# Experts taken in an order that the chip sorts by their tokens, four of them in blocks of 64 tokens

## The chip, the core and the metric

The kernel runs on one core of a Trainium2 chip. The metric is device time in microseconds (us) for one execution, taken as the median over runs.

## What is computed

A float32 network of two blocks over 256 tokens of width 1024. The first block has two layers of a token mixer and a feed-forward part; the feed-forward part of the second layer is a mixture of eight experts, of which each token takes two. All that the change touches lies there:

```python
def _moe(h, w_router, w_gate, w_up, w_down):          # h: 256 tokens x 1024
    logits = (h @ w_router).astype(jnp.float32)
    top_val, top_idx = lax.top_k(logits, TOP_K)        # TOP_K = 2 of N_EXPERTS = 8
    ...
    for e in range(N_EXPERTS):                         # w_gate[e], w_up[e]: 1024 x 2816
        out = out + gates[..., e:e + 1] * _swiglu(h, w_gate[e], w_up[e], w_down[e])
```

`_swiglu` is `(silu(h @ w_gate) * (h @ w_up)) @ w_down`. All weights lie in HBM in float32: 3 x 1024 x 2816 x 4 bytes, 34.6 MB, for each expert.

## The kernel before

**Split operands.** Every float32 operand of a large product is split into a rounded part (`hi`, the type float32r) and the rest (`lo`). A product is then three matmuls into one PSUM bank (`mm3`, L383 to L386): hi by hi, hi by lo, lo by hi. The weights are split when they arrive: ScalarE casts `whi` from the raw tile (L368), VectorE subtracts and writes `wlo` (L370). There are four buffers of each, and one holds two pieces of 128x512 elements; a piece is 256 KB in HBM, and an expert has 132 of them.

**Loads.** SP issues all weight loads on one queue, one behind the other: `fetch` (L290, tiles of 1 MB, `raw`) and `rows_of` (L303, four single pieces of 256 KB, `rawrow`, in buffers that other stages leave free). A load waits until VectorE has split what its buffer held before. Nine loads are asked for before the router runs.

**The experts.** `moe` runs the router, then `prepare(e)` and the expert's products for e = 0 to 7, in that order, for every expert with room for 128 tokens. `route` builds a one-hot matrix `oh` from each token's place in its expert (`R`) and gathers the tokens by matmul (`pgat`, L1279); `prepare` splits them (`xehl`, `xehi`, `xelo`). `hidden` takes the 2816 columns in six groups (five of 512, one of 256): eight steps of 128 rows by three matmuls for gate and again for up (`pgu`), silu, product (`eh`), four transposes (`phT`) and a split (`ehh`, `ehl`). The tokens' split parts are what the array holds and the weights stream through it, so a matmul's length doesn't depend on how many of the 128 tokens are used. `combine` multiplies by the down weights, 2 halves of 22 steps by three matmuls (`pe`), and puts the result back by the transposed one-hot matrix (`psc`). The next expert is prepared in the midst of `hidden` (`then`). The scheduler of the framework places the instructions on each engine.

**More than 128 tokens.** If an expert has more than 128 tokens (`cint`, read by all engines, L1385), a loop over all eight experts (L1387) computes what is left over.

Of the kernel before, what the change touches and what calls it, by code (L numbers as in the profile page):

```python
# [9 lines left out]
F32 = mybir.dt.float32  # L10
F32R = mybir.dt.float32r
# [8 lines left out]
FF = 2816  # L20
# [12 lines left out]
SPREAD = "rcrmrcrmr"  # L33

# [28 lines left out]
def tile_hybrid_stack(ctx: ExitStack, tc: tile.TileContext, a, out, stages=STAGES):  # L63
# [34 lines left out]
    def small(shape, dt=F32, name="s", tag=None):  # L98
        n = 1
        for v in shape[1:]:  # L100
            n *= v
        tag = tag or ("s8" if n <= 8 else "s64" if n <= 64 else "s256")
        bufs = {"s8": 24, "s64": 8, "s256": 3, "kpe": 2, "adac": 10, "adaA": 3, "moe": 2, "moeb": 1, "dtv": 4, "pick": 3,
                "cint": 1}[tag]
        return sm.tile(shape, dt, tag=tag, bufs=bufs, name=nm(name))
# [124 lines left out]
    gp.memset(nones, -1.0)  # L230
    anti = cmat("anti", 1.0, 0.0, [[1, 128]], ALU.is_equal, -127, 1)
# [51 lines left out]
    lent = [False]  # L283

    def fetch(src, r0, nk, c0, n, tag=None):
        if tag is None:
            turn[0] += 1
            tag = "rawb" if turn[0] % 5 in (1, 3) and isinstance(src.offset, int) and not lent[0] else "rawa"
# [19 lines left out]
    def raw_tile(src, r0, nk, c0, n):  # L308
        if isinstance(src.offset, int):
# [30 lines left out]
    def wkey(src, r0, nk, c0, n):  # L340
        return src.tensor.name, src.offset, r0, nk, c0, n
# [846 lines left out]
    def moe(A, B, grow, before_branch):  # L1188
        wg, wu, wd = a["moe_w_gate"][0], a["moe_w_up"][0], a["moe_w_down"][0]
        for e in range(NE):  # L1190
            for c0 in range(0, FF, 512):
                for src in (wg, wu):
                    n = min(512, FF - c0)
                    reqs(src[e], 8, c0, n, STEP[n])
            for hf in range(2):
                reqs(wd[e], FF // P, hf * 512, 512, 4)
# [51 lines left out]
        cint = small([128, 1], I32, name="cint", tag="cint")  # L1248

        def gates():  # L1250
# [11 lines left out]
            cmax = small([128, 1], name="cmax")  # L1262
            vec.tensor_reduce(cmax, pr[:, 2, :], axis=AX.X, op=ALU.max)
            vec.tensor_copy(cint, cmax)

        def route(rcol, gcol, base, more=None):

            oh = pt([128, 2, 128], name="oh")
            for t in range(2):
                vec.tensor_scalar(oh[:, t, :], iota, float(base), rcol(t), op0=ALU.add, op1=ALU.is_equal)  # L1270
# [3 lines left out]
            for b in range(2):  # L1274
                ps = bank((128, 4, 128), "pgat", "o")
# [5 lines left out]
                f = pt([128, 4, 128], name="xe")  # L1281
# [20 lines left out]
        def prepare(e):  # L1302
            oht, gs, fulls = route(lambda t: R[:, t, e:e + 1], lambda t: G[:, t, e:e + 1], 0,
                                  None if e else gates)
            if e % 2:
                return oht, gs, [split(f, [128, 4, 128], "xe") for f in fulls]
# [7 lines left out]
            return oht, gs, xe  # L1314

# [30 lines left out]
        def combine(src, hs, oht, gs):  # L1346
# [23 lines left out]
        for e in range(NE):  # L1370
# [7 lines left out]
            hs = hidden((wg[e], wu[e]), cur[2], then)  # L1378
            combine(wd[e], hs, cur[0], cur[1])
# [5 lines left out]
        most = nc.values_load(cint[0:1, 0:1], min_val=0, max_val=256)  # L1385
        with tc.If(most > 128):
            with tc.For_i(0, NE, 1) as e:  # L1387
                oht, gs, fulls = route(lambda t: R[:, t, 0:1], lambda t: G[:, t, 0:1], 128)
# [4 lines left out]
                for c in (R, G):  # L1393
# [3 lines left out]
                    vec.tensor_copy(c, nx)  # L1397

# [595 lines left out]
```

## Time and profile before

| | |
|---|---|
| median of 3 runs | 2044.44 us (2044.15 to 2050.39) |
| the profiled execution | 2050.83 us, its span 2049.1 us |
| busy in the span: TensorE, VectorE, ScalarE | 1975.2, 1634.5, 1272.8 us |
| moved by DMA | 496.33 MB, mean 242 GB/s |

The span runs from the first to the last instruction. In the profile PE is TensorE's matmuls, DVE VectorE, ACT ScalarE, POOL GpSimd, SPq the queue of SyncE; L368 is a line of the kernel. A busy share over the span is a mean over stages with different limits, so the stage of the experts is looked at by itself.

### The profile page before, as it was taken

The numbers are of one execution on the slowest core, as the hardware profiler recorded it, in microseconds if no ns is written. First come the engines' busy times: TensorE is split into PE (matmuls) and PEld (weight loads), VectorE is DVE, ScalarE is ACT, GpSimd is POOL, SyncE is SP. The second block draws the span as 40 slices with busy tenths as digits, with TensorE's granted clock in tenths as the row PEclk, the third lists the DMA queues.
The fourth block names the chain that finished last, engine by engine and source line by source line (L and its number), as shares of the span: only waits on it lengthen the run. The fifth ranks groups of instructions, "written<-read, shape, count | busy, mean of one in ns | idle before, by whom it ended". The sixth has DMA issues, their size and how long they took to land. (4 is left out here: it accounts for less than half of the span.)

```text
span 2049.1 us, 32577 instructions
## 1 busy us (share of the span) xinstructions
PE 1975.2 (96%) x12095; PEld 1733.4 (85%) x12095; DVE 1634.5 (80%) x2629; ACT 1272.8 (62%) x1962; POOL 131.5 (6%) x207
## 2 busy tenths in 40 slices
PE   6989999998999999999999999989999889999999
PEld 6868998785788888888888888879998779999997
DVE  7888888775699999999999999877668567556783
ACT  2564444456488888788888888755555556545662
POOL 2310000022000000000000000012012000000000
PEclk9998999999899999999999999999999989999999
DMA  9726989662399999999999989845534324554552
GB/s 319 246 92 237 316 306 337 210 196 82 128 327 365 336 371 331 363 329 372 324 379 325 381 313 383 315 126 172 160 124 146 102 74 133 171 183 161 186 167 101
DMA packets 281353, 496.33 MB, mean 242 GB/s; under 512 B 16394, under 2 KB 64852, under 8 KB 281188
## 3 DMA queue, kind: packets, MB, share of 16 engines
q1 hardware_dynamic: 276900, 491.79, 69.1%
q10 hardware_dynamic: 3648, 2.14, 0.4%
q8 instruction: 97, 1.59, 0.3%
q0 software_dynamic: 640, 0.26, 0.1%
q14 instruction: 68, 0.56, 0.1%
HBM read 493.06 MB, written 1.06 MB: 241 GB/s over the span
## 5 line engine op out<-in xcount | busy, mean ns | idle before, releaser
L370 DVE TENSOR_TENSOR wlo<-raw,whi 128x1024 fp32r<-128x1024 f32 (+1 forms) x621 | 749.4, 1219 | 210.0 <-ACT whi L368 202.8
L368 ACT CAST whi<-raw 128x1024 fp32r<-128x1024 f32 (+1 forms) x621 | 647.6, 1048 | 382.8 <-PE pf L480 151.3
L478 PE MATMUL pf<-hhi,whi 128*128 128x256 f32 x1248 | 358.0, 287 | 0.5 <-ACT bc L1646 0.5
L481 PE MATMUL pf<-hhi,wlo 128*128 128x256 f32 x1248 | 357.0, 287 | 0.8 <-DVE wlo L370 0.7
L480 PE MATMUL pf<-hlo,whi 128*128 128x256 f32 x1248 | 356.2, 286 | 0.0
L368 ACT CAST whi<-rawrow 128x512 fp32r<-128x512 f32 x428 | 244.0, 620 | 51.6 <-PE pgu L386 25.6
L370 DVE TENSOR_TENSOR wlo<-rawrow,whi 128x512 fp32r<-128x512 f32 x428 | 270.5, 686 | 0.1
L478 PEld LDWEIGHTS pf<-hhi,whi 128*128 128x128 f32 x1248 | 240.5, 193 | 6.9 <-issue 4.8
L481 PEld LDWEIGHTS pf<-hhi,wlo 128*128 128x128 f32 x1248 | 239.7, 193 | 5.6 <-issue 3.7
L480 PEld LDWEIGHTS pf<-hlo,whi 128*128 128x128 f32 x1248 | 240.6, 193 | 1.8 <-issue 1.5
L385 PE MATMUL pgu<-wlo,xehi 128*128 128x512 f32 (+1 forms) x384 | 144.1, 376 | 0.9 <-DVE wlo L370 0.9
L385 PE MATMUL pgu<-wlo,xehl 128*128 128x512 f32 (+1 forms) x384 | 144.6, 376 | 0.0
L386 PE MATMUL pgu<-whi,xehl 128*128 128x512 f32 (+1 forms) x384 | 142.9, 373 | 0.0
L386 PE MATMUL pgu<-whi,xelo 128*128 128x512 f32 (+1 forms) x384 | 142.7, 372 | 0.0
L384 PE MATMUL pgu<-whi,xehi 128*128 128x512 f32 (+1 forms) x384 | 139.0, 374 | 1.4 <-ACT whi L368 1.4
L384 PE MATMUL pgu<-whi,xehl 128*128 128x512 f32 (+1 forms) x384 | 139.6, 374 | 0.0
L385 PE MATMUL pe<-wlo,ehh 128*128 128x512 f32 x352 | 138.0, 392 | 0.1
L386 PE MATMUL pe<-whi,ehl 128*128 128x512 f32 x352 | 137.1, 389 | 0.0
L384 PE MATMUL pe<-whi,ehh 128*128 128x512 f32 x352 | 136.5, 392 | 0.0
L532 DVE SCALAR_TENSOR_TENSOR acc<-raw,ccol,acc 128x512 f32<-128x512 f32 x164 | 121.9, 749 | 6.7 <-DMA raw<-in_ada_w_dram 4.8
L384 PE MATMUL pt<-whi,hhi 128*128 128x256 f32 (+2 forms) x384 | 115.3, 302 | 0.0
L386 PE MATMUL pt<-whi,hlo 128*128 128x256 f32 (+2 forms) x384 | 114.8, 299 | 0.0
(512 smaller groups left out, 3709.8 us busy)
## 6 DMA issues: line engine op xcount, KB each, us to landing
raw<-in_w_in_dram SPq DMA_DIRECT2D x62, 1024.0 KB
raw<-in_moe_w_up_dram SPq DMA_DIRECT2D x53, 1024.0 KB
raw<-in_moe_w_gate_dram SPq DMA_DIRECT2D x51, 1024.0 KB
raw<-in_moe_w_down_dram SPq DMA_DIRECT2D x45, 1024.0 KB
raw<-in_ada_w_dram SPq DMA_DIRECT2D x44, 1024.0 KB
rawrow<-in_moe_w_gate_dram SPq DMA_DIRECT2D x148, 256.0 KB
rawrow<-in_moe_w_up_dram SPq DMA_DIRECT2D x140, 256.0 KB
rawrow<-in_moe_w_down_dram SPq DMA_DIRECT2D x140, 256.0 KB
```

What stands on the lines that cost most here:

```text
L368: behind("hi", nc.scalar.copy(hi[:, i, :], r), 2)
L370: behind("lo", vec.tensor_sub(lo[:, i, :], r, hi.bitcast(F32)[:, i, :]), 2)
L384: mm(ps, lh, wh, start=first, stop=False, skip_group_check=True)
L385: mm(ps, lh, wl, start=False, stop=False, skip_group_check=True)
L386: mm(ps, ll, wh, start=False, stop=last, skip_group_check=True)
L478: mm(o, wh[j][:, s], X.h(kc), start=(kc == 0 and ch % 2 == 0), stop=False, skip_group_check=True)
L480: mm(o, wh[j][:, s], X.l(kc), start=False, stop=False, skip_group_check=True)
L481: mm(o, wl[j][:, s], X.h(kc), start=False, stop=(kc == KC - 1), skip_group_check=True)
L532: behind("ada", vec.scalar_tensor_tensor(acc, raws[k], ccol[:, k:k + 1], acc, op0=ALU.mult, op1=ALU.add))
```

## The change

Expert 0 is computed first, as before. Its routing gives the number of tokens of each expert, and some 30 small VectorE operations rank experts 1 to 7 by it (`turns_of_experts`). They are then computed in the order of ranks 3, 0, 4, 1, 5, 2, 6 (`TURNS`; rank 0 has the most tokens), so that an expert of the four with the fewest tokens and one of the three with the most take turns. SP reads the seven numbers into registers, and each load of these experts takes its address from such a register.

The four experts of rank 3 to 6 ("light") have room for 64 tokens. The rounded part and the rest of their tokens lie side by side in one operand of 128 columns, so that two matmuls (by `whi` and by `wlo`, `doubled`) stand for three, and rows 0 to 63 and 64 to 127 of the result are two halves that have yet to be added. ScalarE copies each gate and up bank out of PSUM (`eg`), and TensorE adds the halves and transposes in one matmul by a matrix `fold` (128x64, two unit matrices on top of each other). For the down product the same two matmuls are used, and the one-hot matrix, which holds each token twice, adds the halves when it puts tokens back. The loop for what is left over now runs if a heavy expert has more than 128 tokens or a light one more than 64.

```diff
+TURNS = (3, 0, 4, 1, 5, 2, 6)
+HEAVY = 3
...
+    fold = const.tile([128, 64], F32, name="fold")
+    gp.tensor_add(fold, ident[:, 0:64], ident[:, 64:128])
...
-        for e in range(NE):
+        def announce(g, u, d):
...
+        mine = [(wg[0], wu[0], wd[0])]
+        announce(*mine[0])
...
+        def turns_of_experts():
+
+            N = NE - 1
+            cnt = small([128, 8], name="cnt", tag="order")
+            vec.tensor_copy(cnt, pr[:, 2, :])
+            key = small([128, N], name="key", tag="order")
+            vec.scalar_tensor_tensor(key, cnt[:, 1:8], 8.0, iota[:, 1:8], op0=ALU.mult, op1=ALU.subtract)
...
+            vec.tensor_reduce(rank, cube, axis=AX.X, op=ALU.add)
+
+            for i, k in enumerate(TURNS):
+                vec.tensor_scalar(cube[:, i, :], rank, float(k), None, op0=ALU.is_equal)
...
+            vec.tensor_copy(cint[:, 1:8], who)
...
+            vec.tensor_sub(over[:, 1:8], cnt[:, 1:8], rank)
...
+            for t in range(2):
+                vec.tensor_scalar(Rx[:, t, 0:1], R[:, t, 0:1], -128.0, None, op0=ALU.add)
+                vec.tensor_sub(Rx[:, t, 1:8], R[:, t, 1:8], rank)
+                for o, v in ((Rt, R), (Gt, G)):
+                    vec.tensor_tensor(prod, cube, v[:, t, None, 1:8].to_broadcast([128, N, N]), op=ALU.mult)
+                    vec.tensor_reduce(o[:, t, 1:8], prod, axis=AX.X, op=ALU.add)
+            for i in range(N):
+                e = nc.values_load(cint[0:1, i + 1:i + 2], engines=[mybir.EngineType.SP], min_val=0, max_val=NE - 1)
+                mine.append([w[bass.ds(e, 1)].rearrange("o k n -> (o k) n") for w in (wg, wu, wd)])
+                announce(*mine[-1])
...
-        def route(rcol, gcol, base, more=None):
+        def route(rcol, gcol, more=None, n=128):
...
-                        mm(ps[:, i, :], xn[t][:, kc * P:(kc + 1) * P], oh[:, t, :], start=(t == 0),
+                        mm(ps[:, i, :], xn[t][:, kc * P:(kc + 1) * P], oh[:, t, 0:n], start=(t == 0),
...
+            if light(k):
+                oht, gs, fulls = route(lambda t: Rt[:, t, k:k + 1], lambda t: Gt[:, t, k:k + 1], None, 64)
+                xe = []
+                for f in fulls:
+                    hl = pt([128, 4, 128], F32R, "xel")
+                    nc.scalar.copy(hl[:, :, 0:64], f)
+                    vec.tensor_sub(hl[:, :, 64:128], f, hl.bitcast(F32)[:, :, 0:64])
+                    xe.append(hl)
+                return oht, gs, xe
...
+        def light(k):
+            return k and TURNS[k - 1] >= HEAVY
+
+        def doubled(ps, n, hl, wh, wl, j, kc, KC):
+
+            o = hl[kc // 4][:, kc % 4, :]
+            mm(ps[:, :n], o, wh[j], start=(kc == 0), stop=False, skip_group_check=True)
+            mm(ps[:, :n], o, wl[j], start=False, stop=(kc == KC - 1), skip_group_check=True)
+
+        def hidden_light(srcs, xe, then):
...
+                            doubled(ps, n, xe, wh, wl, j, k0 + j, 8)
+                    o = pt([128, 512], name="eg")
+                    nc.scalar.copy(o[:, :n], ps[:, :n])
+                    both.append(o)
+
+                pT = bank((128, 2, 4, 64), "phT", "t")
+                for k in range(2):
+                    for i in range(m):
+                        mm(pT[:, k, i, :], both[k][:, i * P:(i + 1) * P], fold, start=True, stop=True)
+                s = pt([128, 4, 64], name="eh")
+                act(s[:, :m, :], pT[:, 0, :m, :], AF.Silu)
+                vec.tensor_mul(s[:, :m, :], s[:, :m, :], pT[:, 1, :m, :])
+                hl = pt([128, 4, 128], F32R, "ehhl")
+                nc.scalar.copy(hl[:, :m, 0:64], s[:, :m, :])
+                vec.tensor_sub(hl[:, :m, 64:128], s[:, :m, :], hl.bitcast(F32)[:, :m, 0:64])
...
+                        if few:
+                            doubled(ps, 512, hs, wh, wl, j, kc, FF // P)
+                            continue
...
-            hs = hidden((wg[e], wu[e]), cur[2], then)
-            combine(wd[e], hs, cur[0], cur[1])
+            g_, u_, d_ = mine[e]
+            hs = (hidden_light if light(e) else hidden)((g_, u_), cur[2], then)
+            combine(d_, hs, cur[0], cur[1], light(e))
...
-        most = nc.values_load(cint[0:1, 0:1], min_val=0, max_val=256)
+        most = nc.values_load(cint[0:1, 0:1], min_val=0, max_val=384)
+        looped[0] = True
         with tc.If(most > 128):
```

**On SP, at the start of the experts.** Here the queue stands between the first loads of expert 0's gate and up weights and its later ones. Before, one value is read:

```order
L303 DMA rawrow_5768<-in_moe_w_up_dram 128x512
L303 DMA rawrow_5770<-in_moe_w_up_dram 128x512
L1385 TENSOR_LOAD cint_5467
L1385 ISA x2
L290 DMA raw_5797<-in_moe_w_up_dram 128x4x512
```

In the changed kernel seven such reads, each with its two register instructions, come ahead of that one; these are the last two, the old read and the loads behind it:

```order
L1299 TENSOR_LOAD cint_5469
L1299 ISA x2
L1299 TENSOR_LOAD cint_5469
L1299 ISA x2
L1490 TENSOR_LOAD cint_5469
L1490 ISA x2
L296 DMA raw_5910<-in_moe_w_up_dram 128x4x512
L309 DMA rawrow_5932<-in_moe_w_gate_dram 128x512
```

The reads wait for `turns_of_experts`, and the loads of expert 0 that used to follow one read now follow eight. Further on in the same queue, where expert 0's last down weights meet the first weights of the next expert, each load of the latter has a register instruction (ISA) of its own ahead of it:

```order
L309 ISA
L309 DMA rawrow_6620<-in_moe_w_gate_dram 128x512
L296 DMA raw_6592<-in_moe_w_down_dram 128x4x512
L296 ISA
L296 DMA raw_6688<-in_moe_w_gate_dram 128x4x512
```

**On TensorE, in the second expert**, where the first group's up product (`pgu`) is at work. Before, a step is three matmuls:

```order
L384 MATMUL pgu_7101<-whi_7065,xehi_5904 128x512
L385 MATMUL pgu_7101<-wlo_7066,xehi_5904 128x512
L386 MATMUL pgu_7101<-whi_7065,xelo_5906 128x512
L384 MATMUL pgu_7101<-whi_7065,xehi_5904 128x512
L385 MATMUL pgu_7101<-wlo_7066,xehi_5904 128x512
```

In the changed kernel it is two, and the four matmuls by `fold` for the gate bank stand among them:

```order
L1384 MATMUL pgu_6736<-wlo_6721,xel_6017 128x512
L1383 MATMUL pgu_6736<-whi_6739,xel_6020 128x512
L1469 MATMUL psc_6651<-eys_6648,oht_5518 128x512
L1469 MATMUL psc_6655<-eys_6648,oht_5518 128x512
L1405 MATMUL phT_6785<-fold,eg_6734 128x64 x4
L1383 MATMUL pgu_6800<-whi_6763,xel_6017 128x512
L1384 MATMUL pgu_6736<-wlo_6740,xel_6020 128x512
L1383 MATMUL pgu_6736<-whi_6739,xel_6020 128x512
```

`pgu_6800` is the next group's gate bank: its first matmul already stands ahead of the last ones of this group.

**On ScalarE, at the same place.** Before, the silu of the gate bank (`eh`) stands between the casts of weights:

```order
L368 CAST whi_6638<-raw_6632 128x1024
L1331 ACTIVATE eh_6686<-pgu_6576 128x512
L368 CAST whi_6662<-rawrow_6654 128x512
L368 CAST whi_6662<-rawrow_6656 128x512
L368 CAST whi_6668<-rawrow_6658 128x512
```

In the changed kernel two copies (`eg`) and the silu of the folded bank do:

```order
L374 CAST whi_6743<-raw_6737 128x1024
L1399 COPY eg_6734<-pgu_6687 128x512
L374 CAST whi_6763<-rawrow_6755 128x512
L374 CAST whi_6763<-rawrow_6757 128x512
L374 CAST whi_6769<-rawrow_6759 128x512
L374 CAST whi_6769<-rawrow_6761 128x512
L374 CAST whi_6803<-raw_6801 128x1024
L374 CAST whi_6807<-raw_6801 128x1024
L1399 COPY eg_6783<-pgu_6736 128x512
L374 CAST whi_6821<-raw_6819 128x1024
L1407 ACTIVATE eh_6794<-phT_6785 128x256
```

A copy waits for the last matmul of its bank, and the silu for the matmuls by `fold`; the casts behind them on ScalarE wait too.

## Rows read from the trace of the kernel before

**Rows 1.** The page, part 1: busy us (share of the span) and instructions.

```profile
PE 1975.2 (96%) x12095; PEld 1733.4 (85%) x12095; DVE 1634.5 (80%) x2629; ACT 1272.8 (62%) x1962; POOL 131.5 (6%) x207
```

**Rows 2.** Stretches from each expert's first gate matmul to the next one's: busy us, clock, DMA.

```profile
core 0: us, PE busy (x) PEld busy (x) DVE busy (x) ACT busy (x) POOL busy (x), PEclk, DMA share, GB/s
...
952.10:1051.70 99.60, 99.60 (x493) 84.04 (x492) 93.66 (x123) 80.65 (x114) 0.00 (x0) 1.00 0.98 352
...
sum 791.40, PE 788.98 PEld 663.41 DVE 741.57 ACT 637.76 POOL 0.00; mean PE 98.62 PEld 82.93 DVE 92.70 ACT 79.72 POOL 0.00
```

**Rows 3.** Waits in 952.1 to 1051.7 us: us in total, times, longest.

```profile
ACT whi L368 <- PE pgu L386: 8.8, 24, 0.7
...
DVE wlo L370 <- ACT whi L368: 2.9, 7, 0.7
```

**Rows 4.** The same for SP's queue.

```profile
SPq L290 <- DVE wlo L370: 43.4, 20, 6.5
```

**Rows 5.** Groups on PE in the same stretch: count, busy us, mean ns.

```profile
L1279 PE MATMUL pgat<-oh,xn 128*128 128x128 f32 x32 | 3.8, 275 | 0.0
L1335 PE MATMUL phT<-ident,eh 128*128 128x128 f32 x22 | 3.4, 272 | 0.0
```

**Rows 6.** Timeline of PE: start, length; ten matmuls from first to last row.

```profile
1039.65 0.39 PE L386 MATMUL pe<-whi,ehl 128*128 128x512 f32 x1
...
1041.69 0.39 PE L386 MATMUL pe<-whi,ehl 128*128 128x512 f32 x1
```

**Rows 7.** Groups on DVE in 952.1 to 1051.7 us.

```profile
L1340 DVE TENSOR_TENSOR ehl<-phT,ehh 128x512 fp32r<-128x512 f32 x5 | 3.4, 684 | 0.0
L1332 DVE TENSOR_TENSOR eh<-eh,pgu 128x512 f32<-128x512 f32 x5 | 3.4, 682 | 0.5 <-PE pgu L386 0.5
...
L1340 DVE TENSOR_TENSOR ehl<-phT,ehh 128x256 fp32r<-128x256 f32 x1 | 0.4, 421 | 0.0
L1332 DVE TENSOR_TENSOR eh<-eh,pgu 128x256 f32<-128x256 f32 x1 | 0.4, 412 | 0.0
```

**Rows 8.** Groups on ACT in the same stretch.

```profile
L1331 ACT ACTIVATE eh<-pgu 128x512 f32<-128x512 f32 x5 | 3.0, 594 | 0.0
L1338 ACT CAST ehh<-phT 128x512 fp32r<-128x512 f32 x5 | 2.9, 577 | 0.0
...
L1331 ACT ACTIVATE eh<-pgu 128x256 f32<-128x256 f32 x1 | 0.4, 387 | 0.0
...
L1338 ACT CAST ehh<-phT 128x256 fp32r<-128x256 f32 x1 | 0.4, 364 | 0.0
```

**Rows 9.** A stretch in the first mixer, columns as in rows 2.

```profile
15.00:35.00 20.00, 15.26 (x68) 14.66 (x68) 19.24 (x39) 3.86 (x7) 2.85 (x5) 1.00 1.06 383
```

**Rows 10.** Line L1385: count, ns min/median/max, first and last start.

```profile
L1385 SPq TENSOR_LOAD <-cint x1: 472/472/472, 549.8 to 549.8; - x1
...
L1385 SPq FUSED_REGOPS  x1: 178/178/178, 550.4 to 550.4; - x1
```

**Rows 11.** Timeline of SP at the start of the experts.

```profile
562.56 0.38 SPq L290 DMA_DIRECT2D raw<-in_moe_w_up_dram  x1
```

**Rows 12.** Timeline of DVE there: start, length, idle before it and releaser.

```profile
549.65 0.15 DVE L1264 CAST cint<-cmax 128x1 int32<-128x1 f32 x1
553.97 0.41 DVE L1287 TENSOR_SCALAR xe<-pgat,A,adac 128x128 f32<-128x128 f32 x1 [4.17 <-PE pgat L1279]
...
560.14 2.39 DVE L370 TENSOR_TENSOR wlo<-raw,whi 128x1024 fp32r<-128x1024 f32 x2 [0.26 <-ACT whi L368]
```

**Rows 13.** Later stretches, columns as in rows 2.

```profile
1610.00:1615.00 5.00, 3.56 (x23) 2.01 (x24) 2.86 (x7) 1.11 (x2) 0.00 (x0) 0.76 0.00 0
1615.00:1620.00 5.00, 3.78 (x17) 2.27 (x18) 1.08 (x2) 1.46 (x3) 0.00 (x0) 0.50 0.00 0
```

**Rows 14.** Timeline of PE at the lower clock.

```profile
156.13 0.63 PE L385 MATMUL pt<-wlo,mhi 128*128 128x512 f32 x1
156.56 0.63 PE L384 MATMUL pt<-whi,mhi 128*128 128x512 f32 x1
```

More of the change, by code (lines that the diff above doesn't have):

```diff
@@ L103, in small @@
         bufs = {"s8": 24, "s64": 8, "s256": 3, "kpe": 2, "adac": 10, "adaA": 3, "moe": 2, "moeb": 1, "dtv": 4, "pick": 3,
-                "cint": 1}[tag]
+                "cint": 1, "order": 6, "sort": 2}[tag]
         return sm.tile(shape, dt, tag=tag, bufs=bufs, name=nm(name))
@@ L282, in tile_hybrid_stack @@
     RAW = {"rawa": 3, "rawb": 2}
-    lent = [False]
+    lent, looped = [False], [False]
     def fetch(src, r0, nk, c0, n, tag=None):
@@ L287, in fetch @@
             turn[0] += 1
-            tag = "rawb" if turn[0] % 5 in (1, 3) and isinstance(src.offset, int) and not lent[0] else "rawa"
+            tag = "rawb" if turn[0] % 5 in (1, 3) and not looped[0] and not lent[0] else "rawa"
         raw = wraw.tile([128, nk, n], F32, tag=tag, bufs=RAW[tag], name=nm("raw"))
@@ L340, in wkey @@
     def wkey(src, r0, nk, c0, n):
-        return src.tensor.name, src.offset, r0, nk, c0, n
+        return src.tensor.name, src.offset if isinstance(src.offset, int) else id(src), r0, nk, c0, n
     def weights(*req):
@@ L1274, in route @@
             for b in range(2):
-                ps = bank((128, 4, 128), "pgat", "o")
+                ps = bank((128, 4, n), "pgat", "o")
                 for i in range(4):
@@ L1300, in route, with prepare @@
             return oht, gs, fulls
[L1302 to L1306, printed above, removed]
+        def prepare(k):
+            if light(k):
[7 more added lines that the diff above has]
+                return oht, gs, xe
+            r, g = (Rt, Gt) if k else (R, G)
+            oht, gs, fulls = route(lambda t: r[:, t, k:k + 1], lambda t: g[:, t, k:k + 1], None if k else gates)
+            if k == 0:
+                turns_of_experts()
             xe = []
@@ L1314, in prepare @@
             return oht, gs, xe
+        def light(k):
[5 more added lines that the diff above has]
+        def hidden_light(srcs, xe, then):
+            hs = []
+            for c0 in range(0, FF, 512):
+                n = min(512, FF - c0)
+                m = n // P
+                both = []
+                for src in srcs:
+                    ps = bank(name="pgu")
+                    for k0 in range(0, 8, STEP[n]):
+                        wh, wl = weights(src, k0 * P, STEP[n], c0, n)
+                        for j in range(STEP[n]):
+                            doubled(ps, n, xe, wh, wl, j, k0 + j, 8)
[12 more added lines that the diff above has]
+                vec.tensor_sub(hl[:, :m, 64:128], s[:, :m, :], hl.bitcast(F32)[:, :m, 0:64])
+                hs.append(hl)
+                if c0 == 1024:
+                    then()
+            return hs
         def hidden(srcs, xe, then):
@@ L1344, in hidden, with combine @@
             return hs
-        def combine(src, hs, oht, gs):
+        def combine(src, hs, oht, gs, few=False):
             for hf in range(2):
@@ L1392, in moe @@
                 combine(one[2], hs, oht, gs)
-                for c in (R, G):
+                for c in (Rx, G):
                     nx = small([128, 2, 8], name="nx")
@@ L1397, in moe @@
                     vec.tensor_copy(c, nx)
+        looped[0] = False
     def second_columns():
```

37 lines of the change are left out of this document (26 added, 11 removed).

## The prediction

> **What bounds the kernel now.** The page comes first: TensorE is busy for 96% of the span [rows 1]. That alone decides little, since it is a mean over stages, so the stage of the experts is cut into stretches, each from one expert's first gate matmul to the next one's [rows 2]. The eight take 791.4 us together, 98.9 us each on average. In the stretch shown TensorE is busy for all of its 99.6 us at the full clock, VectorE for 93.7 us, ScalarE for 80.7 us, and DMA brings 352 GB/s. The reader should see that TensorE is the limit, but that VectorE stands only 6% behind it. The waits say the same: ScalarE waits for TensorE to give a weight buffer back 24 times for 8.8 us in all, VectorE hardly waits [rows 3], and SP waits 43.4 us for VectorE to empty raw tiles [rows 4], so loads are there before they are wanted. A cheaper matmul therefore gains time only until VectorE, ScalarE or the loads become the limit.
>
> **The light experts' floor on each engine.** Ten 128x512 matmuls in a row start within 2.04 us, nine steps of 0.227 us [rows 6]. A light expert drops 80 of 240 such matmuls for gate and up and 44 of 132 for down, 28.1 us, and 16 of half that width, some 1.8 us. The 22 transposes, 3.4 us [rows 5], become 44 products by `fold`. Those are float32, as the gather is, whose 16 products give 32 rows of 3.8 us in all [rows 5]; 88 rows at no more than 0.12 us cost up to 10.5 us. TensorE needs at most 99.6 - 28.1 - 1.8 - 3.4 + 10.5 = 76.8 us.
> VectorE splits the same weights. The product `eh` and the split `ehl` shrink from 512 to 256 columns a row, 682 to 412 ns and 684 to 421 ns, five times each [rows 7]: 93.7 - 1.4 - 1.3 = 91.0 us. I count no gain on the narrow group.
> ScalarE gets ten wide copies and two narrow ones, priced as the silu from PSUM at 594 and 387 ns, 6.7 us; silu and cast shrink to 387 and 364 ns, five times each, -2.1 us [rows 8]: 80.7 + 6.7 - 2.1 = 85.3 us.
> The loads stay 34.6 MB. Between 15 and 35 us the queue held 383 GB/s with VectorE busy for 19.24 us of 20 [rows 9]; at that rate an expert takes 90.3 us. The Trainium skill (DMA: Bandwidth & Descriptors, Where 436 GB/s comes from) says that HBM gives one core about 358 GB/s and that this side limits a transfer from HBM. By that a light expert would take 96.6 us, and the sum below would end near 2033; the stretch at 383 GB/s doesn't agree with it.
>
> So a light expert lies between 91.0 us (VectorE without a pause) and 98.9 us (no gain). Where VectorE is the limit now, it is busy 19.24 / 20 = 96.2% [rows 9]. I take that: 91.0 / 0.962 = 94.6 us, 4.3 us less, four times: **-17.2 us**.
>
> **The heavy experts.** Four experts prepare a light one while their own products run, and TensorE limits them. The gather then has 64 columns instead of 128; its 3.8 us [rows 5] can fall to between 1.9 us and 3.8 us. I take 1 us each: **-4 us** (0 to -7.6). The tokens' number changes nothing else, since the weights stream.
>
> **The sort.** Some 30 small VectorE operations come in. VectorE stood idle for 4.17 us at that place, until 553.97 us [rows 12], so about half of them, at the 0.15 us of the cast they resemble [rows 12], are covered by the gather on TensorE. The rest, up to 15 x 0.15 = 2.3 us, stand ahead of the first weight split at 560.14 us; behind them wait the split, TensorE's next matmuls and SP. SP reads eight values instead of one, each 0.472 + 0.178 us [rows 10], 4.6 us more. Before, it read at 549.8 us and then had nothing to issue until 562.56 us [rows 11]. With the sorted order ready near 558 to 559 us the reads end near 564 us, 2 us late. The nine loads already there cover it: their 36 pieces last 24 us at three steps of 0.227 us a piece [rows 6]. If that cover were gone, the whole 4.6 us would show. I take **+2 us** (0 to +6).
> Each later load has one register instruction ahead of it, 0.178 us [rows 10]; with some 72 loads an expert that is 13 us of SP's time, hidden in the 43 us in which SP waits anyway [rows 4]. The order of the experts moves whole stages and costs nothing by itself. What stands behind the experts is the same work on every queue.
>
> **The sum.** -17.2 - 4 + 2 = -19.2 us. The profiled execution took 2050.83 us (2049.1 us and 1.7 us around the span), which gives 2031.6 us; the runs shown have their median 6.4 us lower, at 2044.44 us, and the prediction is for that: **2025 us**. With a light expert at 91 to 97 us and the other terms at their ends the case reaches from 2005 to 2043; its own range is 2012 to 2038.
>
> **The rivals.**
> *The time stays.* VectorE, ScalarE and the loads lie within 6 us of each other, and each works behind the others in a fixed order. If their hand-offs eat the gain, a light expert stays near 98.9 us and -4 + 2 = -2 us is left: 2042 us. The same comes out if the loads can't go beyond the 352 GB/s of [rows 2], since 34.6 MB then take 98.3 us. For it: the small distance. Against it: 383 GB/s for 20 us [rows 9], and VectorE's few waits [rows 3].
> *ScalarE becomes the limit (slower).* In a light expert twelve copies, six silus and six casts wait for TensorE or VectorE in ScalarE's queue, with the casts of the next weights behind them. If each of the 24 costs 0.7 us, the longest wait of that kind now [rows 3], ScalarE needs 85.3 + 16.8 = 102.1 us: 4 x 3.2 - 2 = +11 us, 2055 us. It makes the kernel measurably slower from 0.65 us a hand-off. Against it: a copy stands behind a cast that needs a buffer which the same bank's last matmuls give back, so its wait is over when its turn comes.
> *TensorE's clock falls (slower).* TensorE would be busy for 76.8 / 94.6, 81% of a light expert. Between 1610 and 1620 us it was busy 73% and the clock went from 1.00 to 0.50 [rows 13]; there a 512-column step takes 0.43 us [rows 14], 1.9 times as long. With half the work at the lower level a light expert takes 111 us, +46 us: 2091 us. It decides from a third of the work at that level. Against it: 15 to 35 us, busy 76% at a clock of 1.00 [rows 9]; there the pauses are short, as a wait for the next weights would be. The Trainium skill (TensorE: Matmul & The Clock Gate, A second HAM failure mode: psum-queue depth-cycling) tells of a kernel in which short, frequent pauses between groups of matmuls were enough to make the clock swing; by that rule this rival would be the likely one, and 15 to 35 us doesn't agree.
> *The change doesn't do what it says.* If a light expert has more than 64 tokens, the loop for what is left over runs through all eight experts: some 790 us more, 2830 us. By the reference's own routing of its default inputs experts 0 to 7 have 42, 60, 86, 83, 71, 62, 46 and 62 tokens; the light four have 62, 62, 60 and 46, so the loop stays out, by a margin of two tokens.
>
> **Chances.** The forecast 0.72, the time stays 0.12, ScalarE 0.07, the clock 0.05, the loop 0.04. The range leaves out the clock, the loop, ScalarE beyond some +6 us, and the forecast's lowest end: 2006 to 2050 us. About 0.3%, 6 us, can be told from no change here. Faster by more: the forecast without its upper end, 0.70. Within it: that end and the second case, 0.14. Slower: the other three, 0.16.
>
> **What the profile of the changed kernel would show.** Right: the stretches take turns, light ones near 95 us with VectorE busy above 95%, TensorE below 80% and at a clock of 1.00, heavy ones near 98 us with TensorE at 100%; VectorE's waits for DMA stay under 2 us; SP's next load after the eight reads comes near 564 us; the loop's lines don't show. Wrong: VectorE below 92% in a light expert, with waits on ScalarE (hand-offs) or on raw tiles (loads); a clock below 0.9; heavy experts longer than before, because the loads come late into them. The forecast falls if a light expert takes more than 98 us or less than 91 us.

## The result, and the profile after

The changed kernel takes 2009.52 us (median of four runs, 2007.4 to 2011.03) where the kernel before takes 2045.24 us beside it: a ratio of 0.982, with a 95% interval of 0.9807 to 0.9832. That is 35.7 us less, where 19.2 us were forecast. The time lies in the stated range of 2006 to 2050 us, 3.5 us from its lower end, and below the forecast's own range of 2012 to 2038 us.

The profiled execution took 2009.38 us against 2050.83 us, 41.4 us less. The experts' stage, from the first gate matmul of expert 0 to the last matmul of the last expert's down product, went from 791.4 us [rows 2] to 751.0 us: 40.4 us. It began 3.9 us earlier, and 2.9 us came back behind it. In the kernels below its start lies anywhere between 552.4 and 558.7 us, so the first can't be laid to the change; of the 2.9 us some 1.0 can, since a light last expert is put back 4.0 us behind its last down matmul and a heavy one 2.9 us. The stage's 40.4 us are 4.7 us more than the medians differ by. The profiled execution of the kernel before lies 6.4 us above its median, so a term read from one execution of each kernel is good to a few us only.

The page's first part shows little, as it did before [rows 1]:

```profile
PE 1907.2 (95%) x11799; PEld 1648.3 (82%) x11799; DVE 1616.2 (80%) x2660; ACT 1266.6 (63%) x2010; POOL 133.4 (7%) x208
```

The stretches by expert answer to [rows 2], with the same columns. They take turns: positions 1, 3, 5, 7 are light, the others heavy.

```profile
core 0: us, PE busy (x) PEld busy (x) DVE busy (x) ACT busy (x) POOL busy (x), PEclk, DMA share, GB/s
553.00:651.00 98.00, 97.99 (x482) 81.58 (x482) 90.94 (x134) 79.56 (x115) 0.00 (x0) 1.00 0.87 310
651.00:736.90 85.90, 81.31 (x414) 63.69 (x413) 84.53 (x117) 78.43 (x125) 0.00 (x0) 1.00 1.01 363
736.90:839.50 102.60, 100.87 (x496) 84.20 (x495) 97.14 (x136) 80.20 (x115) 0.00 (x0) 1.00 0.99 360
839.50:928.50 89.00, 83.05 (x418) 64.12 (x416) 87.53 (x121) 79.87 (x128) 0.00 (x0) 1.00 1.02 372
928.50:1029.40 100.90, 100.45 (x492) 83.74 (x491) 94.23 (x125) 80.17 (x115) 0.00 (x0) 1.00 1.01 366
1029.40:1118.60 89.20, 83.58 (x416) 63.24 (x415) 87.80 (x121) 78.98 (x127) 0.00 (x0) 1.00 1.00 360
1118.60:1217.50 98.90, 98.58 (x484) 82.26 (x483) 92.45 (x124) 78.16 (x114) 0.00 (x0) 1.00 1.00 363
1217.50:1304.00 86.50, 81.86 (x382) 59.65 (x380) 84.42 (x112) 75.93 (x119) 0.00 (x0) 1.00 1.01 365
sum 751.00, PE 727.70 PEld 582.47 DVE 719.04 ACT 631.29 POOL 0.00; mean PE 90.96 PEld 72.81 DVE 89.88 ACT 78.91 POOL 0.00
```

The four light stretches (85.9, 89.0, 89.2, 86.5) have a mean of 87.7 us, in which VectorE is busy for 98% and TensorE for 93 to 95%. The four heavy ones (98.0, 102.6, 100.9, 98.9) have 100.1 us, with TensorE at 98 to 100%. The clock is 1.00 in all eight. The limit thus changes hands at each expert's border, and a pair takes 187.8 us in place of 197.9 us.

The waits in the light stretch 839.5 to 928.5 us (total, times, longest) turn [rows 3] round: TensorE and its weight loads now wait for VectorE's rests, VectorE waits 1.3 us in all, and a copy from PSUM waits once.

```profile
PEld pe L1384 <- DVE wlo L376: 8.4, 14, 1.6
...
PE pe L1384 <- DVE wlo L376: 3.1, 6, 1.1
...
DVE wlo L376 <- ACT whi L374: 1.3, 3, 0.6
ACT eg L1399 <- PE pgu L1384: 1.3, 1, 1.3
```

SP's queue there, against [rows 4]: the wait of the 1 MB loads for VectorE's rests shrinks from 43.4 to 12.0 us, and SP's waits for transfers to land grow from 9.0 to 21.3 us in all. The queue is full, and the loads still come in time: from the second expert on VectorE waits 0.2 us for them.

```profile
SPq L296 <- DVE wlo L376: 12.0, 7, 4.3
SPq L309 <- DMA raw<-in_moe_w_gate_dram: 9.0, 5, 2.2
```

On TensorE, groups of a light and of the next heavy stretch against [rows 5]: the 88 rows by `fold` at 0.12 us each, 10.9 us and a little over the bound of 10.5, and the gather with 64 columns. It costs what it cost with 128.

```profile
L1405 PE MATMUL phT<-fold,eg 128*128 128x64 f32 x88 | 10.9, 269 | 0.0
...
L1330 PE MATMUL pgat<-oh,xn 128*128 128x64 f32 x32 | 3.7, 271 | 0.0
```

TensorE as a whole was forecast to need at most 76.8 us in a light stretch, and is busy for 81.3 to 83.6 us; a part of that is matmuls that come late for want of `wlo` and look longer (412 and 430 ns in the mean, where those by `whi` take 396 and 395).

VectorE's and ScalarE's groups of the light stretch against [rows 7, 8] are as priced. ScalarE's total isn't: in the profile an instruction begins before the one ahead of it has ended, so that groups of 86.9 us in all keep it busy for 79.9 us, not for the 85.3 forecast.

```profile
L1411 DVE TENSOR_TENSOR ehhl<-eh,ehhl 128x256 fp32r<-128x256 f32 x5 | 2.1, 415 | 0.0
L1408 DVE TENSOR_TENSOR eh<-eh,phT 128x256 f32<-128x256 f32 x5 | 2.1, 412 | 0.0
...
L1399 ACT COPY eg<-pgu 128x512 f32<-128x512 f32 x10 | 5.8, 591 | 1.3 <-PE pgu L1384 1.3
```

At the sort, against [rows 10, 11]: seven register loads (min/median/max in ns), and SP's next load.

```profile
L1299 SPq TENSOR_LOAD <-cint x7: 262/262/470, 554.4 to 558.1; - x7
L1299 SPq FUSED_REGOPS  x7: 147/147/178, 555.0 to 558.4; - x7
...
559.30 0.38 SPq L296 DMA_DIRECT2D raw<-in_moe_w_up_dram  x1
```

That load stands 6.3 us behind expert 0's first gate matmul at 553.03 us; before, it was 562.56 - 556.89 = 5.7 us. Expert 0's stretch grew from 97.3 to 97.9 us.

### The profile page after: what moved, and what is told of

It reads as the page before. It is cut to its first block, busy times and chain, and to the rows that moved or that the text cites. A ratio compares the mean times of both kernels' runs of the same rounds, so it can differ in the third digit from the quotient of the medians.

```text
span 2007.7 us, 33037 instructions
## 1 busy us (share of the span) xinstructions
PE 1907.2 (95%) x11799; PEld 1648.3 (82%) x11799; DVE 1616.2 (80%) x2660; ACT 1266.6 (63%) x2010; POOL 133.4 (7%) x208
## 5 line engine op out<-in xcount | busy, mean ns | idle before, releaser
L374 ACT CAST whi<-raw 128x1024 fp32r<-128x1024 f32 (+1 forms) x621 | 640.5, 1049 | 356.6 <-PE pf L486 150.0
L1384 PE MATMUL pgu<-wlo,xel 128*128 128x512 f32 (+1 forms) x384 | 148.0, 398 | 7.9 <-DVE wlo L376 6.5
L1383 PE MATMUL pgu<-whi,xel 128*128 128x512 f32 (+1 forms) x384 | 138.6, 376 | 0.0
L391 PE MATMUL pt<-wlo,hhi 128*128 128x256 f32 (+2 forms) x384 | 113.9, 297 | 0.0
L1384 PEld LDWEIGHTS pgu<-wlo,xel 128*128 128x128 f32 x384 | 72.3, 188 | 40.6 <-DVE wlo L376 30.1
L391 PEld LDWEIGHTS pgu<-wlo,xehl 128*128 128x128 f32 x384 | 72.4, 189 | 17.7 <-DVE wlo L376 5.4
L1384 PE MATMUL pe<-wlo,ehhl 128*128 128x512 f32 x176 | 74.7, 425 | 12.5 <-DVE wlo L376 12.1
```

Source lines behind the costliest of these rows:

```text
L374: behind("hi", nc.scalar.copy(hi[:, i, :], r), 2)
L391: mm(ps, lh, wl, start=False, stop=False, skip_group_check=True)
L1383: mm(ps[:, :n], o, wh[j], start=(kc == 0), stop=False, skip_group_check=True)
L1384: mm(ps[:, :n], o, wl[j], start=False, stop=(kc == KC - 1), skip_group_check=True)
```

## The experiments

All ratios are to the kernel before, run beside each kernel. "Against the change" is the ratio less 0.982, times 2045.24 us; a difference of some 4 us can't be told from none, and the intervals of the three kernels at +5.5 to +7.0 us overlap that of the changed one. "Stage" is the experts' part of the profiled execution.

| kernel | median us | ratio (95%) | against the change | stage us |
|---|---|---|---|---|
| before | 2045.24 | | | 791.4 |
| changed | 2009.52 | 0.982 (0.9807 to 0.9832) | | 751.0 |
| sort_only | 2046.45 | 0.9999 (0.9983 to 1.0014) | +36.6 | 790.6 |
| fixed | 2017.16 | 0.9856 (0.9834 to 0.9877) | +7.4 | 758.7 |
| grouped | 2024.46 | 0.9889 (0.9867 to 0.9912) | +14.1 | 765.8 |
| all_light | 1995.81 | 0.9757 (0.9734 to 0.978) | -12.9 | 740.0 |
| vector_more | 2025.22 | 0.9889 (0.9861 to 0.9916) | +14.1 | 765.1 |
| vector_less | 2007.77 | 0.9818 (0.9795 to 0.9842) | -0.4 | 748.3 |
| pool_splits | 2017.02 | 0.9854 (0.9825 to 0.9883) | +7.0 | 755.4 |
| fewer_loads | 2011.64 | 0.9821 (0.9791 to 0.9852) | +0.2 | 750.3 |
| first_light | 1999.49 | 0.9758 (0.9728 to 0.9789) | -12.7 | 741.7 |
| grouped_late | 2015.84 | 0.9848 (0.9825 to 0.9872) | +5.7 | 758.0 |
| after_late | 2015.32 | 0.9847 (0.983 to 0.9864) | +5.5 | 755.3 |
| first_late | 2001.3 | 0.9782 (0.9765 to 0.9799) | -7.8 | 742.4 |

### Which part gives the gain: sort_only and fixed

sort_only:

```diff
-HEAVY = 3
+HEAVY = 7
```

> All experts heavy, sorted order and register addresses kept (capacity 128 for all). If the whole gain comes from the two matmuls in place of three, this run shows only the price of the sort: +0.6 us (97.3 to 97.9 us in expert 0's stretch) to +2 us (the prediction's term), so 2045 to 2047.5 us, ratio 1.000 to 1.001. Rival: the loads through registers, or the other order of the experts, gave part of the 40 us themselves; then this run is 10 us or more under the kernel before. A second rival, that the 72 register instructions an expert cost time which the light experts' gain covers, gives 5 us or more over it.

No difference from the kernel before can be measured, and the stage is 790.6 against 791.4 us. The sort, the register loads, the register instruction ahead of each load and the other order of the experts neither gain nor cost 3 us together. The gain is the light path's.

fixed:

```diff
+FIXED = (0, 5, 2, 7, 3, 1, 4, 6)
-            for i in range(N):
-                e = nc.values_load(cint[0:1, i + 1:i + 2], engines=[mybir.EngineType.SP], min_val=0, max_val=NE - 1)
+        for f in FIXED[1:]:
+            mine.append((wg[f], wu[f], wd[f]))
```

> The changed kernel's order written into the program (experts 0, 5, 2, 7, 3, 1, 4, 6), without the sort and with constant addresses; the loop then covers only experts of more than 128 tokens, none here. By the prediction's sort term it is 2 us faster than the changed kernel (2007.5 us), by the stretch of expert 0 in its trace 0.6 us (2009 us). Rival: the register instruction ahead of every load delays SP, which now waits for DMAs and raw tiles in turn; then it is 5 us or more faster.

It is slower, which no theory had. Expert 0's stretch is 97.2 us, 0.7 us under the changed kernel's; but sort_only, which sorts too, has 96.7 us there against 97.3 us before, so the sort's price can't be told from nothing. Nothing is won by constant addresses either: the first seven experts take 664.2 us, in the changed kernel 664.5 us. The loss lies elsewhere: in the last expert, 94.3 us against 86.5 us, where the loads fall to 314 GB/s and the clock to 0.96 in the mean (columns as above).

```profile
1220.70:1315.00 94.30, 86.47 (x388) 63.83 (x387) 86.67 (x116) 78.53 (x122) 0.00 (x0) 0.96 0.88 314
```

In it ScalarE stands in front of a copy until TensorE is through the bank, and the next cast behind it (start, length, and the idle time before):

```profile
1275.02 0.59 ACT L1364 COPY eg<-pgu 128x512 f32<-128x512 f32 x1 [2.50 <-PE pgu L1349]
...
1276.58 2.36 DVE L377 TENSOR_TENSOR wlo<-raw,whi 128x1024 fp32r<-128x1024 f32 x2 [2.62 <-ACT whi L375]
```

VectorE, behind the cast, stands for as long, and so the raw tiles come free late and the loads stop. Why it comes to this here and not in the changed kernel, whose queues carry the same work, stays open.

### Does a light expert have a limit of its own: all_light and grouped

all_light:

```diff
-HEAVY = 3
+HEAVY = 0
-            vec.tensor_scalar(rank, rank, 64.0, 64.0, op0=ALU.mult, op1=ALU.add)
+            vec.tensor_scalar(rank, rank, 64.0, 128.0, op0=ALU.mult, op1=ALU.add)
```

> All of experts 1 to 7 take the light way; the tokens beyond 64 of the three experts that have more (86, 83 and 71) are left out, and the loop for them stays out. It shows a light expert's own limit. Theory 1 (VectorE's 87.4 us of work at 98% busy, 89 us): the stage is 98 + 7 x 89 = 721 us, 30 us under the changed kernel, 1980 us. Theory 2 (light ones gain from heavy neighbours, alone 92 to 95 us): 98 + 7 x 93.5 = 752 us, no gain over the changed kernel. If the loads are the limit (34.6 MB at 360 to 372 GB/s, the light stretches' rate) a light expert takes 93 to 96 us, with VectorE under 95% busy and waiting for DMA; at 388 GB/s, 89 us.

It lies between the theories. The seven light experts take (740.1 - 97.9) / 7 = 91.7 us, VectorE busy for (705.26 - 90.88) / 7 = 87.8 us of it; the last number is a light expert's work on VectorE, for which 91.0 was forecast. The first four of the seven hold the stall that grouped shows below; the last three take 91.3, 88.2 and 90.3 us.

```profile
834.60:927.00 92.40, 84.52 (x412) 63.77 (x411) 87.12 (x121) 79.38 (x126) 0.00 (x0) 0.98 1.04 378
...
sum 740.10, PE 690.82 PEld 526.87 DVE 705.26 ACT 632.75 POOL 0.00; mean PE 86.35 PEld 65.86 DVE 88.16 ACT 79.09 POOL 0.00
```

grouped:

```diff
-TURNS = (3, 0, 4, 1, 5, 2, 6)
+TURNS = (3, 4, 5, 6, 0, 1, 2)
```

> The same work as the changed kernel, but the four light experts stand together (positions 1 to 4) and the heavy ones behind them (5 to 7). Theory 1, each kind has its own limit (light: VectorE's work, some 87.4 us at 98% busy, 89 us; heavy: TensorE's 98.9 us): the stage stays at 750 us within 4 us, the whole at 2009 us. Theory 2, a light expert takes 86 to 89 us only because VectorE works ahead, and the loads come ahead, during the heavy neighbour: light ones in a row take 92 to 95 us, heavy ones 98.9 us in place of 100.1, and the stage grows by 4 x 5.5 - 4 x 1.2 = +17 us (12 to 25): about 2027 us.

Theory 2's size came: +14.8 us in the stage, with light stretches of 90.5, 93.4, 92.3 and 94.1 us. But half of its reason falls. The first light expert has the same heavy neighbour in both kernels and does the same work, up to the preparation of the next expert; it takes 90.5 us against 85.9. The place where they part is ScalarE's queue behind the gather. In the changed kernel the copies `eg` come next (start, length, idle before):

```profile
695.08 0.37 ACT L1345 CAST oht<-poh 128x256 fp32r<-128x256 f32 x1 [2.92 <-PE poh L1343]
695.35 0.59 ACT L1399 COPY eg<-pgu 128x512 f32<-128x512 f32 x1
...
696.78 0.60 ACT L1399 COPY eg<-pgu 128x512 f32<-128x512 f32 x1
697.25 0.48 ACT L1336 ACTIVATE xe<-pgat,adac,A 128x128 f32<-128x128 f32 x1
```

In the grouped kernel, where a light expert prepares a light one, the scheduler put the tokens' pieces ahead of them; ScalarE, VectorE and TensorE in turn:

```profile
698.40 0.37 ACT L1345 CAST oht<-poh 128x256 fp32r<-128x256 f32 x1 [2.82 <-PE poh L1343]
...
699.82 0.40 ACT L1336 ACTIVATE xe<-pgat,adac,A 128x64 f32<-128x64 f32 x1
...
705.41 0.41 ACT L1360 CAST xel<-xe 128x256 fp32r<-128x256 f32 x1
705.72 1.07 ACT L1399 COPY eg<-pgu 128x512 f32<-128x512 f32 x2
...
709.71 1.23 DVE L376 TENSOR_TENSOR wlo<-raw,whi 128x1024 fp32r<-128x1024 f32 x1 [2.61 <-ACT whi L374]
...
706.36 1.10 PE L1405 MATMUL phT<-fold,eg 128*128 128x64 f32 x8 [3.38 <-ACT eg L1399]
...
708.39 0.63 PE L1384 MATMUL pgu<-wlo,xel 128*128 128x512 f32 x1
```

The copies come 7.3 us behind `oht`, in the changed kernel 0.3 us. TensorE waits 3.38 us for them, gives no weight buffer back meanwhile, and VectorE stands for 2.61 us. Then the matmuls start 0.43 us apart, because the clock has gone to its lower level:

```profile
707.00:709.00 2.00, 2.00 (x10) 1.68 (x9) 0.10 (x1) 0.37 (x1) 0.00 (x0) 0.66 1.05 390
709.00:711.00 2.00, 2.00 (x7) 1.52 (x6) 1.23 (x1) 1.34 (x2) 0.00 (x0) 0.50 1.02 374
711.00:713.00 2.00, 2.00 (x14) 1.82 (x13) 1.49 (x2) 1.70 (x3) 0.00 (x0) 0.99 0.08 30
```

### The place of the copies: grouped_late, after_late and first_late

The edit, made in three kernels, writes the preparation one group later inside a light expert, behind that group's two copies; so they stand ahead of it in ScalarE's queue.

```diff
+                if c0 == 1536:
+                    then()
                 pT = bank((128, 2, 4, 64), "phT", "t")
...
-                if c0 == 1024:
-                    then()
```

> The grouped order again (lights at positions 1 to 4), with the preparation of the next expert written one group later inside a light expert, behind the two PSUM copies (eg) of that group. In the grouped kernel ScalarE's queue has oht, four xe, two xel and only then the copies, in the changed kernel oht and then the copies. If that place of the copies is what made light experts in a row take 92.6 us (TensorE waited 3.4 us for eg there, and the clock fell to 0.50 for some 4 us), they take 87.6 to 89 us now and the kernel ends near 2010 us. If a light expert needs a heavy neighbour to lend it time, nothing changes: 2024 us.

> The changed kernel with the same shift of the preparation inside its light experts. There the copies already stand ahead of the tokens' pieces, so by the theory of the copies' place nothing changes: 2009.5 us, within 4 us. If the preparation's place costs by itself, 4 us or more either way.

> Expert 0 light as well (the version of 1999.5 us), with the same shift. One light expert there prepares a light one, and one more has a part of its preparation ahead of a copy (90.0 us against 85.6 to 87.3 us). By the theory of the copies' place it gains about 1 x 4 + 1 x 2 us: 1993 to 1996 us. By the rival, no change.

In the grouped order the shift gives back 7.8 of the 14.8 us of the stage, and the ratio says 8.4 us. Light experts in a row then take 88.8, 90.2, 92.5 and 91.1 us, 90.6 in the mean, VectorE busy for 88.2 us or 97%; two of them:

```profile
743.09:833.25 90.16, 84.35 (x418) 63.66 (x417) 88.27 (x131) 78.91 (x126) 0.00 (x0) 1.00 1.04 375
833.25:925.75 92.50, 85.15 (x419) 63.42 (x418) 91.03 (x125) 80.33 (x129) 0.00 (x0) 1.00 1.04 378
```

The 3.0 us that are left to the changed kernel's 87.7 us aren't the neighbours' alone, since the shift was made as well. The run to compare with is after_late, which has the same shift in the alternating order. Its light experts take 88.3 us in the mean and its heavy ones 100.5 us; in grouped_late it is 90.6 and 98.9 us. A light and a heavy stretch of after_late:

```profile
847.00:934.28 87.28, 81.53 (x409) 64.46 (x408) 83.53 (x116) 78.21 (x125) 0.00 (x0) 0.98 1.05 381
934.28:1037.28 103.00, 102.26 (x499) 84.74 (x499) 98.06 (x130) 81.66 (x118) 0.00 (x0) 1.00 0.99 357
```

What a light expert gains beside heavy ones, 2.3 us, the heavy ones give back for the most part, 1.6 us. The two stages differ by 2.7 us and the two ratios by 0.2 us, which can't be told from none. So of the 14.8 us between grouped and the changed kernel, 7.8 us go with the place of the copies and 4.3 us with what the shift itself costs; that the order gains anything by itself isn't shown.

after_late and first_late missed: the one is 5.5 us slower than the changed kernel (4.3 in the stage), so the preparation's place seems to cost by itself; the other is no faster than first_light. So the place of the copies isn't the whole story. In first_light the seventh expert, a light one that prepares a light one, has the same order in the queue, pieces before copies, and takes 87.1 us without such a wait; ScalarE's wait for the gather was 0.76 us there, not 2.82. The order lets a stall happen; that it depends on how late ScalarE is is argued from these two waits. In after_late a new one came at 715 us, in which ScalarE stood for 2.7 us with no cause that the trace shows; grouped_late has one of 2.1 us in the same place.

### What limits a light expert: vector_more, vector_less, pool_splits, fewer_loads

vector_more:

```diff
+                for _ in range(3):
-                vec.tensor_sub(hl[:, :m, 64:128], s[:, :m, :], hl.bitcast(F32)[:, :m, 0:64])
+                    vec.tensor_sub(hl[:, :m, 64:128], s[:, :m, :], hl.bitcast(F32)[:, :m, 0:64])
```

> The changed kernel with the rest of each hidden piece of a light expert (ehhl, 415 ns on VectorE) computed three times over instead of once: 2 x (5 x 0.415 + 0.28) = 4.7 us more VectorE work in each of four light experts, nothing else. If VectorE's work is what limits a light expert, even beside heavy neighbours, all of it shows: 4 x 4.7 = +19 us (15 to 21), 2028 us. If the loads limit it, or TensorE's hand-offs, VectorE has slack and it shows less than +6 us.

+14.1 us by the ratio and in the stage, just under the 15 to 21 expected: 3.5 us of the 4.7 added to each light expert show. The sum row of its eight stretches has VectorE at 734.50 us, 15.5 us more than the changed kernel's 719.04. Two things besides VectorE's load may be in the 14.1 us: in the first light stretch ScalarE stood for 3.4 us with no cause that the trace shows, and the repeated work delays pieces that TensorE needs (it waited for one of them for 1.9 us).

vector_less:

```diff
-                nc.scalar.copy(hl[:, :m, 0:64], s[:, :m, :])
-                vec.tensor_sub(hl[:, :m, 64:128], s[:, :m, :], hl.bitcast(F32)[:, :m, 0:64])
+                nc.scalar.copy(hl[:, :m, :].rearrange("p m (k s) -> p m k s", k=2),
+                               s[:, :m, None, :].to_broadcast([128, m, 2, 64]))
```

> The changed kernel, with the rests of a light expert's hidden pieces left out: ScalarE writes the rounded piece into both halves, in one copy of 512 columns (577 ns in place of 408 ns), so the rounded part counts twice there. VectorE has 5 x 0.415 + 0.28 = 2.4 us less in each light expert. If VectorE limits light experts and nothing else stands close behind: 4 x 2.4 = 9.4 us less, 2000 us. If the hand-offs between ScalarE and TensorE stand right behind VectorE: less than half of that, 2005 us or more.

Nothing by the ratio, 2.7 us in the stage. VectorE had 712.30 us to do, 6.7 less, and 4 of them turned into waits for ScalarE's casts. The first row is of the changed kernel from 650 to 1310 us, the second of vector_less from 650 to 1300 us:

```profile
DVE wlo L376 <- ACT whi L374: 11.7, 27, 0.9
```

```profile
DVE wlo L376 <- ACT whi L374: 15.6, 36, 1.0
```

So VectorE is the limit from above, with the hand-offs from TensorE through ScalarE right behind it: more work shows for the most part, less work hardly at all. ScalarE's wider copy (590 ns against 394 in the mean, 24 times, 4.8 us) may be a part of that.

pool_splits:

```diff
-                    vec.tensor_sub(hl[:, :, 64:128], f, hl.bitcast(F32)[:, :, 0:64])
+                    gp.tensor_sub(hl[:, :, 64:128], f, hl.bitcast(F32)[:, :, 0:64])
-                vec.tensor_sub(hl[:, :m, 64:128], s[:, :m, :], hl.bitcast(F32)[:, :m, 0:64])
+                (vec if n < 512 else gp).tensor_sub(hl[:, :m, 64:128], s[:, :m, :], hl.bitcast(F32)[:, :m, 0:64])
```

> The changed kernel with the rests of the hidden pieces and of the tokens of a light expert (ehhl of 512 wide groups, xel) computed on GpSimd instead of VectorE: 5 x 0.415 + 2 x 0.42 = 2.9 us less VectorE work in each light expert. If VectorE's work is the limit: 4 x 2.9 = 11.6 us less, 1998 us. If the loads are the limit: no change, within 3 us. Rival: GpSimd is so much slower that what waits for it, or VectorE's own instructions beside it, give the gain back: 2009 us or more, with VectorE's groups longer or waits on GpSimd in the trace.

The rival is right in that nothing is won: 7.0 us slower by the ratio, 4.4 us in the stage. GpSimd takes 2.7 us a piece in the mean (its spans are rough), and VectorE's busy time is 719.04 us, as much as with the pieces. Its weight splits, of which nothing was changed, took 5.6 us more in all (from 650 to 1310 us). GpSimd's group, two of its pieces, and VectorE: beside the short piece four weight splits of 512 columns took 3.02 us, without GpSimd 2.48 us, and under the first part of the long one 2.49 us.

```profile
L1411 POOL TENSOR_TENSOR ehhl<-eh,ehhl 128x256 fp32r<-128x256 f32 x20 | 54.5, 2724 | 382.7 <-ACT ehhl L1410 367.3 <-DMA rawrow<-in_moe_w_down_dram 15.4
```

```profile
859.17 9.87 POOL L1411 TENSOR_TENSOR ehhl<-eh,ehhl 128x256 fp32r<-128x256 f32 x1 [62.24 <-ACT ehhl L1410]
870.60 1.25 POOL L1411 TENSOR_TENSOR ehhl<-eh,ehhl 128x256 fp32r<-128x256 f32 x1 [1.56 <-ACT ehhl L1410]
```

```profile
858.99 2.49 DVE L376 TENSOR_TENSOR wlo<-rawrow,whi 128x512 fp32r<-128x512 f32 x4
...
871.18 3.02 DVE L376 TENSOR_TENSOR wlo<-rawrow,whi 128x512 fp32r<-128x512 f32 x4
...
876.39 2.48 DVE L376 TENSOR_TENSOR wlo<-rawrow,whi 128x512 fp32r<-128x512 f32 x4
```

The Trainium skill (GPSIMD Engine Reference, Specifications) says that GpSimd shares its interfaces to SBUF with VectorE and contends with instructions that read two inputs from SBUF, as these do. The row of 3.02 us agrees; the row of 2.49 us shows nothing of it.

fewer_loads:

```diff
-        raw = raw_tile(src, r0, nk, c0, n)
+        raw = thrifty(src, r0, nk, c0, n)
...
+            if sparing[id(src)] % 3 == 0 and last[0] == (id(src), nk, n):
+                last[0] = None
+                return last[1]
```

> The changed kernel with some of the weight tiles of light experts not loaded: where the same matrix was split right before, its raw tile is split once more in place of the next one (57 of 627 loads of the experts left out, some 5 to 9 MB of 34.6 MB in each light expert), so the output is made from the wrong weights there. All work on the engines stays. If the loads limit a light expert (it moves 34.6 MB in 87.6 us, 395 GB/s, more than the 383 GB/s that I took), it gets 10 us or more faster in all: under 2000 us. If VectorE limits it, the time stays within 3 us of the changed kernel's 2009.5 us.

Its light and heavy stretches moved 319 to 358 GB/s where the changed kernel's moved 360 to 372 (positions 1 to 6), and the time is the same. The loads are not the limit, though the queue is full.

### A version for these tokens: first_light

```diff
-TURNS = (3, 0, 4, 1, 5, 2, 6)
+TURNS = (0, 3, 1, 4, 2, 5, 6)
-            return k and TURNS[k - 1] >= HEAVY
+            return k == 0 or TURNS[k - 1] >= HEAVY
```

> Expert 0, which has 42 tokens here, takes the light way too (a limit of 64 in the overflow test), and the order becomes light, heavy, light, heavy, light, heavy, light, light. By the prediction's own terms each light expert saves 4.3 us whatever stands beside it: 2005 us. If a pair of heavy and light is what counts (187.6 us) and a light expert beside another light one takes 92.6 us, as in the grouped order: 3 x 187.6 + 2 x 92.6 = 748 us against 750.5 us, 2007 us. If every light expert takes 87.6 us: 2009.5 - 11 = 1998 us.

The last case came: 12.7 us less than the changed kernel by the ratio, 10.0 us between the medians, 9.3 us in the stage. Each light expert took 85.6 to 90.0 us, the two that stand together too (the last has nobody to prepare), so they show no price of a light neighbour.

```profile
1126.00:1213.10 87.10, 82.16 (x412) 62.76 (x412) 85.64 (x120) 78.32 (x127) 0.00 (x0) 1.00 1.04 376
1213.10:1300.40 87.30, 81.74 (x380) 58.95 (x378) 85.85 (x115) 75.70 (x119) 0.00 (x0) 1.00 1.05 377
```

It is the fastest version here that computes the whole reference, 2.4% under the kernel before. It needs expert 0 at 64 tokens or fewer; here it has 42.

## Why the prediction held, and what it mis-sized

**The direction and the mechanism were right, the sizes weren't.** Light and heavy stretches take turns, light ones limited by VectorE (98% busy), heavy ones by TensorE, at a clock of 1.00. But a light expert took less than 91 us, which the prediction had named as a sign that it fails, and the gain is 35.7 us, not 19.2. Two more of its signs failed: TensorE was busy for 93 to 95% of a light stretch, not for less than 80%, and the heavy experts became longer, though not by the loads. That the time still lies in the stated range is luck in part. The light experts' term was 27.8 us too small and the heavy ones' erred by 8.8 us the other way; with the heavy term as forecast the kernel would have ended near 2001 us, below the range.

**The term for the light experts, -17.2 us, was mis-sized**: it measured 4 x (87.65 - 98.9) = -45.0 us. The 6.95 us between the forecast 94.6 and 87.65 have three parts. VectorE's work was put at 91.0 us and is 87.8 to 88.2 in the kernels with light experts in a row: I had started from one stretch with 93.66 us where the mean of eight is 92.70 [rows 2], and had counted no gain for the smaller pieces of the tokens and the narrow group. At the same share that is 88.2 / 0.962 = 91.7 us, 2.9 less. The busy share was put at 96.2% and is 97.3% in a row (grouped_late): 90.6 us, 1.1 less. The last 3.0 us lie between grouped_late and the changed kernel: by after_late some 0.7 us of them go with the place of the preparation, and 2.3 us come beside heavy experts. I had treated each expert by itself, but engines run ahead: the light stretches hold 86.1 us of VectorE's work in the mean, not 88.2, and some of it has moved into the heavy ones.

**The heavy experts, -4 us: wrong.** The gather's 64 columns cost 3.7 us, 128 cost 3.8. The term measured 4 x (100.1 - 98.9) = +4.8 us: a heavy expert begins where VectorE has no lead, and TensorE waits there, by the rows above 2.5 us in the three stretches behind light ones; the rest isn't accounted for. That this pays for what the light neighbours gain is argued from these sums; no run took VectorE's lead away alone.

**The sort, +2 us**, measured 0.6 to 0.7 by expert 0's stretch in the changed kernel and in fixed, and nothing by sort_only. The register loads took 262 ns in the median, not 472.

**The rivals.** *The time stays*: the loads were no limit (fewer_loads). The first light stretch, 651.0 to 736.9 us in forty slices, held some 386 GB/s in most of them:

```profile
GB/s 386 386 385 387 385 383 387 387 388 384 389 386 385 389 385 387 374 312 250 372 371 274 72 403 389 359 296 388 277 358 357 398 399 389 385 387 388 383 386 388
```

The limit of about 358 GB/s per core that the Trainium skill states (DMA: Bandwidth & Descriptors, Where 436 GB/s comes from) doesn't agree with this row. *ScalarE* did not become the limit here, but it is the nearest danger: in grouped, all_light and fixed its copies held up all three engines. The rival's price went by [rows 3], which show ScalarE's waits for gate and up alone; with those for the down product it waited 15.2 us there, 43 times and at most 0.8 us. *The clock* stayed at 1.00, and where ScalarE made TensorE wait in grouped it fell for some 4 us, not for half of an expert. It fell as briefly in light stretches of after_late, vector_more, pool_splits and fewer_loads, whose means are 0.96 to 0.98. The Trainium skill's account of frequent short pauses (TensorE: Matmul & The Clock Gate, A second HAM failure mode: psum-queue depth-cycling) doesn't agree with the changed kernel, where TensorE stood for 4.6 to 6.0 us of each light stretch, in waits of at most 1.5 us, at a clock of 1.00. *The loop* stayed out.

## What to carry to other kernels

When the limit changes hands between neighbouring pieces of work, cost the pair and not each piece: an engine that is ahead in one lends time to the next, and what one stretch gains the next gives back in part. Whether alternating kinds gains over grouping them isn't shown here: with the preparation in the same place the two orders came out alike. So change one thing at a time, and compare an edit with a run that has the same edit. Take the work of an engine from the mean over all stretches, not from one. A small copy that TensorE needs, queued behind work that isn't urgent, can stop three engines: look at what stands ahead of it in its queue.

## What the runs showed of the hardware

A float32 gather of 64 columns costs as much as one of 128 (271 and 275 ns a matmul in the profile, 32 of them each). In grouped the clock went from 1.00 to 0.50 after a wait of TensorE of 3.38 us and was back within some 4 us; in after_late it did the same after waits of 0.8 and 1.3 us, and in the changed kernel one of 1.7 us, at 740.6 us, left it at 1.00. GpSimd's subtractions did not unload VectorE: its busy time stayed at 719.04 us, and its weight splits became longer in places (3.02 against 2.48 us for four) and not in others (2.49 us).
